# Gate and up of f-tiles 8 to 15 by seven products of halves, with sums of weights made in DRAM

## The chip, the cores and the metric

The kernel runs on one core of a Trainium2 chip. The metric is the device time of one execution in microseconds; 1120.35 us is the median of three runs of the kernel before (1120.31 to 1120.71).

## The reference

One decoder layer for 512 tokens and 1024 channels, all in float32: half a SwiGLU feed-forward added to x, two attention mixers with gates, an output projection, a second half feed-forward, a final RMSNorm. The change touches the first feed-forward only:

```python
def _swiglu(x, w_gate, w_up, w_down):
    return (jax.nn.silu(x @ w_gate) * (x @ w_up)) @ w_down

h = h + FFN_HALF * _swiglu(_rmsnorm(h, norm_ffn1[i]), ffn1_gate[i], ffn1_up[i], ffn1_down[i])
```

w_gate and w_up are 1024 x 2816, w_down is 2816 x 1024.

## The kernel before

**Layout.** Activations lie transposed: channels in partitions (8 tiles of 128, index d or k), the 512 tokens along the free dimension. The hidden width 2816 is 22 f-tiles of 128, worked in three parts (THIRDS: tiles 0 to 7, 8 to 15, 16 to 21). For each tile a gate and an up product go through TensorE, their SwiGLU is stored in G, and at the end of a third the eight output tiles of the down-projection are added to h.

**Two parts for each operand.** A float32 number is split into a high part (the cast to the matmul's type) and a low part (the rest), and a product is three matmuls: high x high, high x low, low x high. Activations are uh and ul, G holds its high parts in slots j and its low parts in slots 8+j, weights are whi and wlo. So `mm3` with 8 k-tiles is 24 matmuls, each 128 weight columns against 512 moving token columns.

**Weights.** `Weights` plans all blocks in the order of use, 512 KB each (128 x 8 x 128). A block is loaded on SP's queue into one of 4 raw buffers (`load`), split into one of 4 slots of whi and wlo (`split`: ScalarE casts, L142; VectorE subtracts, L146), and taken by `next`, which first prepares the blocks up to AHEAD = 2 further on. A load is issued three blocks ahead of the split, and waits for the split that frees its raw buffer; a cast waits for the matmuls that free its slot. Each engine runs its instructions in the order in which the program lists them.

**SwiGLU.** `swiglu` (L624 to L630, then `split`): z = gate x r_b (the norm's factor) on VectorE, Silu on ScalarE, t = up x r_b and g = s x t on VectorE, the high part of G on ScalarE (L379), the low one on VectorE (L380).

**Between the tiles.** After each tile `side` does a step of small tables (masks, rope tables) and `early` a step for twelve blocks of w_in that are used much later: load to a buffer of their own (eraw), cast and split (L103, L104), store both parts to DRAM. There is one block in each of the three stages at a time. Steps come after each tile and twice in each of the first two down-projections.

**PSUM.** `acc(False)` gives banks named acc, o, s in turn; each name has two buffers. The first matmuls of the mixing stage take both buffers of o, then both of s.

Of the kernel before, what the change touches and what calls it, by code (L numbers as in the profile page):

```python
# [59 lines left out]
class Weights:  # L60
# [19 lines left out]

    def plan(self, ap, nk, early=False, wide=False):
# [44 lines left out]
    def load(self, n):  # L126
        while len(self.raw) <= n and len(self.raw) < len(self.blocks):
            if len(self.raw) in self.stored:
                self.raw.append(None)
                continue  # L130
            ap, nk = self.blocks[len(self.raw)]
            t = self.raw_pool.tile([128, 8, 128], F32, name="raw")
            wide = self.wide[len(self.raw)]
            self.nc.sync.dma_start(t.rearrange("p (a b) c -> p a (b c)", a=2) if wide else t[:, :nk], ap)
            self.raw.append(t)
# [218 lines left out]
def layer(ctx, tc, a, out):  # L354
# [56 lines left out]


    def plan_ffn(n, begun=0, rows=()):
        for f0, f1 in THIRDS:
            for f in range(max(f0, begun), f1):
                for w in ("gate", "up"):
                    W.plan(cols(a[f"ffn{n}_{w}"], DFF, 0, KD, f * 128, 128), KD)
            if rows and f1 < NF:
                for m, g in STEPS:
                    W.plan(quarter(f0, m, g), 8, wide=True)  # L420
                continue
# [143 lines left out]
    def norm_in(d, norm):  # L565
# [4 lines left out]
        square(d)  # L570

    def square(d):
        if d == 0:
            scalar.activation(sqacc, h[:, d], AF.Square)
        else:
            sq = temp.tile([128, S], F32, name="turn_a")
            scalar.activation(sq, h[:, d], AF.Square)  # L577
# [44 lines left out]
    def swiglu(pg, pu, j):  # L622
# [8 lines left out]
        split(G[:, j], G[:, 8 + j], g)  # L631

    def ffn(after, begun, side, sums, early):

# [6 lines left out]
        def rows():  # L641
            norm_rows(norm["col"])
            for j, b in enumerate(begun):
                swiglu(*b, j)

        for third, (f0, f1) in enumerate(THIRDS):
            for f in range(f0 + (len(begun) if f0 == 0 else 0), f1):
                first = f == len(begun)
# [3 lines left out]
                mm3(pu, W.next(), u_in, KD, rows if first else None)  # L652
                swiglu(pg, pu, f - f0)
                next(side, None)
                next(early, None)
            for d in range(KD):
# [4 lines left out]
                vector.scalar_tensor_tensor(h[:, d], po, 0.5, h[:, d], op0=OP.mult, op1=OP.add)  # L661
                if third < 2 and d in (2, 5):
                    next(early, None)
                if third == 2:
                    after(d)


    hd = tc.dram_tile([KD, 128, S], F32, name="hd")

    with pool("h1") as h_pool, pool("temp1", 2) as temp, pool("tables") as tables, ExitStack() as starting:  # L670
# [108 lines left out]
        starting.close()  # L779
        with pool("stage", 2) as stage:  # L780
            ffn(to_mix, begun, side_work(), sums=sums0, early=W.early(stage))


    with ExitStack() as mixing:
        temp = mixing.enter_context(pool("temp2", 2))
# [950 lines left out]
```

## Time and profile before

| | |
|---|---|
| profiled execution | 1120.31 us, span 1118.5 us |
| TensorE (PE) busy | 1103.9 us, 99% of the span |
| VectorE (DVE) busy | 677.5 us, 61% |
| ScalarE (ACT) busy | 473.2 us, 42% |
| GpSimd (POOL) busy | 168.0 us, 15% |
| transfers | 163.16 MB, 146 GB/s in the mean |
| gate and up of f-tiles 8 to 15 | 142.71 to 229.75 us |

In a row of a timeline stand start, duration, engine, line, operation, output <- input; in brackets the idle time before it and what ended it. A row of the chain has start, duration, engine, tile, line and count. The row of a window has its length and, for TensorE's matmuls, its weight loads, VectorE, ScalarE and GpSimd, the busy time and the number of instructions; then the clock, the share of the DMA engines and GB/s. The row of a group has its count, busy time and mean in ns. An instruction of VectorE or ScalarE lasts a little longer than the distance to the next one, since its end overlaps the next one's start.

### The profile page before, as it was taken

The numbers are of one execution on the slowest core, as the hardware profiler recorded it, in microseconds if no ns is written. First come the engines' busy times: TensorE is split into PE (matmuls) and PEld (weight loads), VectorE is DVE, ScalarE is ACT, GpSimd is POOL, SyncE is SP. The second block draws the span as 40 slices with busy tenths as digits, with TensorE's granted clock in tenths as the row PEclk, the third lists the DMA queues.
The fourth block names the chain that finished last, engine by engine and source line by source line (L and its number), as shares of the span: only waits on it lengthen the run. The fifth ranks groups of instructions, "written<-read, shape, count | busy, mean of one in ns | idle before, by whom it ended". The sixth has DMA issues, their size and how long they took to land.

```text
span 1118.5 us, 14865 instructions
## 1 busy us (share of the span) xinstructions
PE 1103.9 (99%) x5571; PEld 933.1 (83%) x5571; DVE 677.5 (61%) x1243; ACT 473.2 (42%) x890; POOL 168.0 (15%) x189
## 2 busy tenths in 40 slices
PE   9999999999999999999999999999999999999997
PEld 7888888888888999998888888888888888888876
DVE  5665447543446578996777546653667754685553
ACT  5444223321234456666666543434334322342332
POOL 0100000000001145654334422120000000000002
PEclk9999999999999999999999999999999999999999
DMA  7387557533225547656658455633234623354312
GB/s 232 95 245 248 185 173 240 171 113 105 84 80 153 139 119 180 161 151 198 197 155 250 108 161 162 173 88 111 76 113 142 196 78 113 111 177 126 91 61 76
DMA packets 200577, 163.16 MB, mean 146 GB/s; under 512 B 6325, under 2 KB 177145, under 8 KB 200441
## 3 DMA queue, kind: packets, MB, share of 16 engines
q1 hardware_dynamic: 192392, 141.09, 41.9%
q0 software_dynamic: 5440, 16.78, 6.6%
q10 hardware_dynamic: 2672, 4.35, 1.0%
q8 instruction: 44, 0.72, 0.3%
q14 instruction: 29, 0.23, 0.1%
HBM read 142.27 MB, written 36.70 MB: 160 GB/s over the span
## 4 chain that ended last, share of the span: by engine, by line
PE 95%; DVE 2%; ACT 1%; issue 1%; POOL 0%; POOLq 0%; DVEq 0%; ACTq 0%
PE acc L376 37%; PE o L376 27%; PE s L376 27%; PE tp L1427 2%; DVE turn_a L1125 0%; PE tp L376 0%; PE tp L1053 0%; PE tp L718 0%; DVE wlo L146 0%; ACT whi L142 0%; PE tp L1624 0%; PE tp L985 0%; DVE s L1333 0%; POOL sqacc L578 0%; DVE sqacc L1170 0%
## 5 line engine op out<-in xcount | busy, mean ns | idle before, releaser
L146 DVE TENSOR_TENSOR wlo<-raw,whi 128x1024 fp32r<-128x1024 f32 (+2 forms) x189 | 214.6, 1163 | 42.3 <-ACT whi L142 42.2
L142 ACT CAST whi<-raw 128x1024 fp32r<-128x1024 f32 (+2 forms) x214 | 190.2, 918 | 109.8 <-PE acc L376 41.7
L376 PE MATMUL acc<-uh,whi 128*128 128x512 f32 x336 | 133.4, 397 | 0.7 <-ACT turn_a L1244 0.7
L376 PE MATMUL acc<-uh,wlo 128*128 128x512 f32 x336 | 131.3, 391 | 0.0
L376 PE MATMUL acc<-ul,whi 128*128 128x512 f32 x336 | 131.1, 390 | 0.0
L376 PE MATMUL o<-uh,whi 128*128 128x512 f32 x264 | 103.7, 393 | 0.5 <-ACT whi L723 0.4
L376 PE MATMUL o<-ul,whi 128*128 128x512 f32 x264 | 102.8, 389 | 0.0
L376 PE MATMUL o<-uh,wlo 128*128 128x512 f32 x264 | 102.8, 389 | 0.0
L376 PE MATMUL s<-uh,whi 128*128 128x512 f32 x232 | 90.5, 390 | 0.0
L376 PE MATMUL s<-uh,wlo 128*128 128x512 f32 x232 | 90.3, 389 | 0.0
L376 PE MATMUL s<-ul,whi 128*128 128x512 f32 x232 | 90.3, 389 | 0.0
L376 PEld LDWEIGHTS acc<-uh,wlo 128*128 128x128 f32 x336 | 63.1, 188 | 13.9 <-DVE wlo L146 0.4
L578 POOL TENSOR_TENSOR sqacc<-sqacc,turn_a 128x512 f32<-128x512 f32 x14 | 18.2, 1300 | 371.1 <-ACT turn_a L577 371.1
L376 PEld LDWEIGHTS acc<-uh,whi 128*128 128x128 f32 x336 | 63.1, 188 | 12.9 <-ACT turn_a L1244 1.1
L376 PEld LDWEIGHTS acc<-ul,whi 128*128 128x128 f32 x336 | 63.2, 188 | 11.9
L376 PE MATMUL acc<-whi,uh 128*128 128x256 f32 x224 | 65.6, 293 | 1.2 <-ACT whi L142 1.2
L379 ACT CAST G<-g 128x512 fp32r<-128x512 f32 x28 | 17.4, 622 | 111.5 <-DVE g L630 82.3
L376 PE MATMUL acc<-wlo,uh 128*128 128x256 f32 x224 | 63.3, 283 | 0.1
L376 PE MATMUL acc<-whi,ul 128*128 128x256 f32 x224 | 63.3, 282 | 0.0
L376 PEld LDWEIGHTS o<-uh,whi 128*128 128x128 f32 x264 | 49.6, 188 | 11.4 <-ACT whi L723 0.9
L376 PEld LDWEIGHTS o<-uh,wlo 128*128 128x128 f32 x264 | 49.5, 188 | 10.5
L376 PEld LDWEIGHTS o<-ul,whi 128*128 128x128 f32 x264 | 49.6, 188 | 10.3
(342 smaller groups left out, 2320.7 us busy)
## 6 DMA issues: line engine op xcount, KB each, us to landing
raw<-in_ffn_gate_dram SPq DMA_DIRECT2D x42, 512.0 KB, 4.0
raw<-in_ffn_up_dram SPq DMA_DIRECT2D x42, 512.0 KB, 5.2
raw<-in_ffn_down_dram SPq DMA_DIRECT2D x34, 512.0 KB, 4.7
t<-in_ffn_down_dram POOLq DMA_DIRECT2D x12, 1024.0 KB, 9.4
raw<-in_w_in_dram SPq DMA_DIRECT2D x20, 512.0 KB, 4.2
raw<-t SPq DMA_DIRECT2D x16, 512.0 KB, 4.4
eraw<-in_w_in_dram SPq DMA_DIRECT2D x12, 512.0 KB, 7.3
early<-ehi SPq DMA_DIRECT2D x12, 512.0 KB, 5.2
```

The lines of the kernel that those rows point to most:

```text
L142: self.nc.scalar.copy(self.place(i)[0][:, k0:k1], self.raw[i][:, k0:k1])
L146: engine.tensor_tensor(lo, self.raw[i][:, k0:k1], f32(hi), op=OP.subtract)
L376: tensor.matmul(out, lhsT, rhs, start=start, stop=stop)
L379: scalar.copy(hi, src)
L578: gpsimd.tensor_tensor(sqacc, sqacc, sq, op=OP.add)
L1427: tensor.transpose(ps[:w, hd], u.p[:, hd, kb * w:kb * w + w], ident)
```

## The change

Tiles 8 to 15 are worked in four units of two tiles. In a unit the matrix of weights is cut in four (gate and up, each by the two halves of the 1024 channels: g0, g1, u0, u1; 256 columns), u is cut in four (the halves of the channels by the halves of the tokens), and the four blocks of the result come from seven products of sums of these, each of 4 k-tiles, 2 column tiles, 3 parts and 256 moving columns: 24 matmuls. `unit` works them in the order 1, 6, 5, 2, 7, 3, 4 in three banks, adds further products into a bank where the sum allows, and combines the banks on VectorE.

- Three products take gate or up weights as they are, four take sums (s1 to s4) that `unit_sums` makes in DRAM: for each group of four tiles eight transfers on GpSimd's queue, 1 MB each, four of them adding into their target. `sums_of_u` makes the sums of u (split in two parts, tiles bhi and blo) while tiles 4 to 7 are worked.
- A unit takes 7 weight blocks (4 k-tiles by 256 columns) where two tiles took 4; AHEAD is 3 within units.
- The low parts of a unit's G are left to the start of the next (`settle`), or to after the last unit's early step.
- The early blocks lose eraw and go through the 4 raw buffers. Their steps come after the last two units, in the down-projection behind them, in the last third and its first two outputs. Side steps also run in the first down-projection.
- The scratch for GpSimd's DMA descriptors is 8192 where it had its default.

```diff
+UNITS = {1: (8, 16)}
+PRODUCTS = 1, 6, 5, 2, 7, 3, 4
+CHUNK = 4
@@ Weights.early @@
-            raw[n] = pool.tile([128, nk, 128], F32, name="eraw")
+            raw[n] = self.raw_pool.tile([128, nk, 128], F32, name="raw")
@@ new: unit_sums @@
+        for f, nf in chunks(UNITS[n]):
+            g0, g1, u0, u1 = (half(n, what, kh, f, nf) for what in ("gate", "up") for kh in range(2))
+            s1, s2, s3, s4 = (sum_tile(n, f, k) for k in range(1, 5))
+            for o, i, add in ((s1, u0, 0), (s3, g0, 0), (s1, u1, 1), (s3, u0, 1), (s2, s1, 0), (s2, g0, 1), (s4, s2, 0),
+                              (s4, g1, 1)):
+                if add:
+                    gpsimd.dma_start(o, i, accum_op=OP.add)
+                else:
+                    gpsimd.dma_start(o, i)
+                yield
@@ new: sums_of_u(n, k), k = 0..3 @@
+        b, p, q = (temp.tile([128, 2, 256], F32, name=name) for name in "zst")
+        scalar.activation(b[:, 0], h12, AF.Identity, scale=g1)
+        scalar.activation(b[:, 1], h22, AF.Identity, scale=g2)
+        vector.scalar_tensor_tensor(p[:, 0], h11, g1, b[:, 0], op0=OP.mult, op1=OP.subtract)
+        vector.tensor_tensor(p[:, 1], b[:, 1], p[:, 0], op=OP.add)
+        vector.tensor_tensor(q[:, 0], b[:, 0], b[:, 1], op=OP.subtract)
+        vector.scalar_tensor_tensor(q[:, 1], h21, g2, p[:, 1], op0=OP.mult, op1=OP.subtract)
+        for i, x in ((0, p), (2, q)):
+            split(both["hi"][:, k, i:i + 2], both["lo"][:, k, i:i + 2], x)
@@ new: unit(j) @@
+        def gated(s, x, i):
+            tt(x, s, x, op=OP.mult)
+            hi, lo = (G[:, b:b + 2, i * 256:i * 256 + 256] for b in (j, 8 + j))
+            scalar.copy(hi, x)
+            owed.append(lambda: tt(lo, x, f32(hi), op=OP.subtract))
+        for m in PRODUCTS:
+            wh, wl = W.next()
+            xh, xl = right(m)
+            ps = banks[home[m]]
+            new = m in (1, 5, 6)
+            for k in range(4):
+                for i in range(2):
+                    o, n = ps[:, i], 2 * k + i
+                    for step, (a_, x) in enumerate(((wh, xh), (wh, xl), (wl, xh))):
+                        tensor.matmul(o, a_[:, n], x(k), start=new and n == step == 0, stop=n == 7 and step == 2,
+                                      skip_group_check=True)
+            if m == 1:
+                settle()
+                scalar.activation(p, ps, AF.Identity, scale=-1.0)
+            if m == 6:
+                tt(u, ps, p, op=OP.add)
+            if m == 5:
+                tt(w, p, ps, op=OP.subtract)
+            if m == 2:
+                tt(z, ps, r0, op=OP.mult)
+                scalar.activation(z, z, AF.Silu)
+            if m == 7:
+                tt(w, ps, w, op=OP.add)
+                tt(w, w, r1, op=OP.mult)
+            if m == 3:
+                tt(u, ps, u, op=OP.subtract)
+                tt(u, u, r1, op=OP.mult)
+                scalar.activation(u, u, AF.Silu)
+            if m == 4:
+                gated(u, w, 1)
+                tt(t, ps, p, op=OP.add)
+                tt(t, t, r0, op=OP.mult)
+                gated(z, t, 0)
@@ ffn @@
+            while f < f1:
+                if lo <= f < hi:
+                    W.AHEAD = 3
+                    unit(f - f0)
+                    W.AHEAD = 2
+                    f += 2
+                    if f > hi - 4:
+                        next(early, None)
+                    continue
...
+                f += 1
+                if third == 0:
+                    if f > 4:
+                        sums_of_u(0, f - 5)
+                        next(adds, None)
+                        next(adds, None)
+                else:
+                    next(early, None)
                 next(side, None)
-                next(early, None)
+            settle()
             for d in range(KD):
...
-                if third < 2 and d in (2, 5):
+                if third == 0:
+                    next(side, None)
+                    next(adds, None)
+                if third == 1 and d % 2 == 0 or third == 2 and d < 2:
                     next(early, None)
@@ kernel @@
-    nc = bacc.Bacc("TRN2", target_bir_lowering=False, num_devices=1)
+    nc = bacc.Bacc("TRN2", target_bir_lowering=False, num_devices=1, dynamic_dma_scratch_size=8192)
```

VectorE within a tile of the second third before (wlo is a weight split, G the low part):

```order
L146 TENSOR_TENSOR wlo<-raw,whi 128x1024 x2
L624 TENSOR_TENSOR z<-o,r_b 128x512
L628 TENSOR_TENSOR t<-s,r_b 128x512
L630 TENSOR_TENSOR g<-s,t 128x512
L380 TENSOR_TENSOR G<-g,G 128x512
```

VectorE in a unit now, from the first operation on product 2 (z) to the last on product 4 (g; the tags of the tiles are p, s = u, t = w, z, g = t of the code; s<-s reads a bank named s):

```order
L745 TENSOR_TENSOR z<-acc,r_b 128x512
L149 TENSOR_TENSOR wlo<-raw,whi 128x1024
L748 TENSOR_TENSOR t<-o,t 128x512
L749 TENSOR_TENSOR t<-t,r_b 128x512
L149 TENSOR_TENSOR wlo<-raw,whi 128x1024
L751 TENSOR_TENSOR s<-s 128x512
L752 TENSOR_TENSOR s<-s,r_b 128x512
L149 TENSOR_TENSOR wlo<-raw,whi 128x1024
L721 TENSOR_TENSOR t<-s,t 128x512
L756 TENSOR_TENSOR g<-o,p 128x512
L757 TENSOR_TENSOR g<-g,r_b 128x512
L721 TENSOR_TENSOR g<-z,g 128x512
```

ScalarE over a whole unit now (whi is the cast of a weight block, z and s the Silu, G the high parts):

```order
L739 ACTIVATE p<-acc 128x512
L145 CAST whi<-raw 128x1024 x3
L746 ACTIVATE z<-z 128x512
L145 CAST whi<-raw 128x1024 x2
L753 ACTIVATE s<-s 128x512
L145 CAST whi<-raw 128x1024
L723 CAST G<-t 128x2x256
L723 CAST G<-g 128x2x256
```

Where two splits and four operations stood for a tile, a split stands after nearly every step of the combination, and the cast of that split stands behind the Silu or the cast of G on ScalarE.

VectorE from the last unit's product 4 into the down-projection now (elo is an early block's low part, h an output of the down-projection):

```order
L721 TENSOR_TENSOR g<-z,g 128x512
L107 TENSOR_TENSOR elo<-raw,ehi 128x1024
L724 TENSOR_TENSOR G<-t,G 128x2x256
L724 TENSOR_TENSOR G<-g,G 128x2x256
L807 SCALAR_TENSOR_TENSOR h<-o,h 128x512
```

The early block's low part moved ahead of the low parts of G for tiles 14 and 15; before, G's low part came right behind g.

SP's queue at the last unit now (the first w_in row is the first early block, the up row behind it the weights of that unit's product 4, s_12_3 and s_12_4 are sums):

```order
L137 DMA raw<-in_ffn_gate_dram 128x4x256
L137 DMA raw<-s_12_3_90 128x4x256
L137 DMA raw<-s_12_4_91 128x4x256
L101 DMA raw<-in_w_in_dram 128x8x128
L137 DMA raw<-in_ffn_up_dram 128x4x256
```

The early block now stands in the same ring of raw buffers, one load ahead of product 4's weights.

More of the change, by code (lines that the diff above doesn't have):

```diff
@@ L79, in __init__, with plan @@
         self.pos = 0
-    def plan(self, ap, nk, early=False, wide=False):
+    def plan(self, ap, nk, early=False, wide=0):
         if early:
@@ L410, in quarter, with half, chunks, sum_tile @@
         return dram(a["ffn2_down"], (f0 + 4 * g + j) * 128 * D + k * 512, [[D, 128], [256 * D, 2], [1, 512]])
+    def half(n, what, kh, f, nf):
+        return dram(a[f"ffn{n}_{what}"], kh * 512 * DFF + f * 128, [[DFF, 512], [1, nf * 128]])
+    def chunks(tiles):
+        return [(f, min(CHUNK, tiles[1] - f)) for f in range(tiles[0], tiles[1], CHUNK)]
+    s_sums = {(n, f + i, k): (tc.dram_tile([512, nf * 128], F32, name="s%d_%d_%d" % (n, f, k)), i) if i == 0 else (f, i)
+              for n, tiles in UNITS.items() for f, nf in chunks(tiles) for i in range(0, nf, 2) for k in range(1, 5)}
+    def sum_tile(n, f, k):
+        t, i = s_sums[n, f, k]
+        return t if i == 0 else s_sums[n, t, k][0]
+    def unit_sums(n):
+        for f, nf in chunks(UNITS[n]):
[8 more added lines that the diff above has]
+                yield
+    def unit_block(n, f, m):
+        if m in (1, 2, 4):
+            what, kh = {1: ("gate", 0), 2: ("gate", 1), 4: ("up", 1)}[m]
+            return cols(a[f"ffn{n}_{what}"], DFF, kh * 512, 4, f * 128, 256)
+        k = {5: 1, 6: 2, 7: 3, 3: 4}[m]
+        c = (f - UNITS[n][0]) % CHUNK * 128
+        return sum_tile(n, f, k).rearrange("(k p) c -> p k c", p=128)[:, :, c:c + 256]
     def plan_ffn(n, begun=0, rows=()):
+        lo, hi = UNITS.get(n, (0, 0))
         for f0, f1 in THIRDS:
             for f in range(max(f0, begun), f1):
+                if lo <= f < hi:
+                    for m in PRODUCTS if (f - lo) % 2 == 0 else ():
+                        W.plan(unit_block(n, f, m), 8, wide=4)
+                    continue
                 for w in ("gate", "up"):
@@ L419, in plan_ffn @@
                 for m, g in STEPS:
-                    W.plan(quarter(f0, m, g), 8, wide=True)
+                    W.plan(quarter(f0, m, g), 8, wide=2)
                 continue
@@ L575, in square @@
         else:
-            sq = temp.tile([128, S], F32, name="turn_a")
+            sq = temp.tile([128, S], F32, name=square_tag[0])
             scalar.activation(sq, h[:, d], AF.Square)
@@ new lines, in right, with settle, unit @@
+    def right(m):
+        if m in (1, 2, 3):
+            d, c = {1: (0, 0), 2: (4, 0), 3: (4, 256)}[m]
+            return tuple((lambda k, x=x: x[:, d + k, c:c + 256]) for x in (uh, ul))
+        i = {5: 0, 6: 1, 7: 2, 4: 3}[m]
+        return tuple((lambda k, x=both[part]: x[:, k, i]) for part in ("hi", "lo"))
+    owed = []
+    def settle():
+        for x in owed:
+            x()
+        owed.clear()
+    def unit(j):
+        banks = {n: psum.tile([128, 2, 256], F32, name=n) for n in ("acc", "o", "s")}
+        home = {1: "acc", 2: "acc", 5: "s", 3: "s", 6: "o", 7: "o", 4: "o"}
+        r0, r1 = (r_b[:, None, c:c + 256].to_broadcast([128, 2, 256]) for c in (0, 256))
+        p, u, w, z, t = (temp.tile([128, 2, 256], F32, name=name, bufs=2 if name != "p" else 1) for name in ("p", "s", "t", "z", "g"))
+        tt = vector.tensor_tensor
+        def gated(s, x, i):
[36 more added lines that the diff above has]
+                gated(z, t, 0)
@@ L665, in ffn @@
                     after(d)
+        for g in (adds, side, early):
+            for _ in g:
+                pass
     hd = tc.dram_tile([KD, 128, S], F32, name="hd")
@@ L779, in layer @@
         starting.close()
-        with pool("stage", 2) as stage:
+        with pool("stage", 2) as stage, pool("both") as sums_pool:
+            both["hi"], both["lo"] = (sums_pool.tile([128, 4, 4, 256], F32R, name=n) for n in ("bhi", "blo"))
             ffn(to_mix, begun, side_work(), sums=sums0, early=W.early(stage))
+    square_tag[0] = "turn_a"
     with ExitStack() as mixing:
```

13 lines of the change are left out of this document (11 added, 2 removed).

## The prediction

> **What bounds the kernel now.** I read the page's shares and its chain first.
>
> ```profile
> span 1118.5 us, 14865 instructions
> PE 1103.9 (99%) x5571; PEld 933.1 (83%) x5571; DVE 677.5 (61%) x1243; ACT 473.2 (42%) x890; POOL 168.0 (15%) x189
> PE 95%; DVE 2%; ACT 1%; issue 1%; POOL 0%; POOLq 0%; DVEq 0%; ACTq 0%
> ```
>
> TensorE carries 95% of the chain, so fewer matmul microseconds are worth something only while the other engines keep up. The sum is made against this execution's own time, 1120.31 us (span 1118.5 and 1.8 around it); the median of the three runs is 1120.35. Next the chain in order of time and the windows, for f-tiles 8 to 15 and the down-projection behind them.
>
> ```profile
> 142.87 5.44 PE o L376 x24
> ...
> 224.47 5.44 PE o L376 x24
> 229.91 5.44 PE s L376 x24
> ```
> ```profile
> 142.71:229.75 87.04, 87.04 (x385) 72.07 (x384) 50.58 (x78) 28.59 (x35) 0.00 (x0) 1.00 0.62 194
> ```
>
> Sixteen groups of 24 matmuls, 5.44 us each without a gap, 87.04 us in all: 226.7 ns per 512-wide matmul. VectorE is busy for 50.6 us (58%) of it, some of that rotary-table side work and early-gate splits, ScalarE for 28.6.
>
> **The matmuls.** A unit (two f-tiles) needs 7 products of 24 matmuls with 256 moving columns, 168, where 96 of 512 stood. The 256-wide pace is taken from a projection of the next stage:
>
> ```profile
> 385.35 8.64 PE acc L376 x72
> L376 PEld LDWEIGHTS acc<-uh,whi 128*128 128x128 f32 x336 | 63.1, 188 | 12.9 <-ACT turn_a L1244 1.1
> ```
>
> 72 in 8.64 us is 120 ns each, with a weight load before every one. So a product takes 2.88 us, a unit 20.16, and before 96 x 0.2267 = 21.76: 1.60 less per unit, 6.4 over four. Bounds: 113 ns (half of the 512-wide), which gives 10.9 less, and 188 ns (the load's own row), which gives 39 more; I take 120, the same width in an unbroken run.
>
> **VectorE and ScalarE in a unit.** This decides. The rows that price a step:
>
> ```profile
> 197.31 0.69 DVE L628 TENSOR_TENSOR t<-o,r_b 128x512 f32<-128x512 f32 x1 [3.13 <-PE o L376]
> 198.10 0.69 DVE L630 TENSOR_TENSOR g<-s,t 128x512 f32<-128x512 f32 x1
> 199.49 0.69 DVE L380 TENSOR_TENSOR G<-g,G 128x512 fp32r<-128x512 f32 x1 [0.69 <-ACT G L379]
> 200.09 0.24 DVE L547 TENSOR_SCALAR m<-n 128x160 f32<-128x160 f32 x1
> ...
> 202.10 2.35 DVE L146 TENSOR_TENSOR wlo<-raw,whi 128x1024 fp32r<-128x1024 f32 x2
> 204.37 0.68 DVE L624 TENSOR_TENSOR z<-s,r_b 128x512 f32<-128x512 f32 x1
> ```
> ```profile
> 198.83 0.62 ACT L379 CAST G<-g 128x512 fp32r<-128x512 f32 x1 [3.93 <-DVE g L630]
> 199.36 1.04 ACT L103 CAST ehi<-eraw 128x1024 fp32r<-128x1024 f32 x1
> ...
> 205.15 0.63 ACT L626 ACTIVATE s<-z 128x512 f32<-128x512 f32 x1 [2.85 <-DVE z L624]
> ```
> ```profile
> 361.26 1.04 ACT L142 CAST whi<-raw 128x1024 fp32r<-128x1024 f32 x1
> 362.33 1.55 DVE L146 TENSOR_TENSOR wlo<-raw,whi 128x1024 fp32r<-128x1024 f32 x1 [0.71 <-ACT whi L142]
> ```
>
> On VectorE a 512-wide operation lets an independent one start 0.60 after it (199.49 to 200.09) and one that needs its result 0.79 after (197.31 to 198.10); two splits and the next operation take 2.27 (202.10 to 204.37), 1.13 each (1.22 for the last). ScalarE takes a result 0.04 (cast) or 0.10 (Silu) after VectorE ends, can start its next instruction 0.53 after such a one, casts a block in 1.05, and VectorE takes that 0.03 later.
>
> A unit puts on VectorE 7 splits, 7.91 us, and 13 operations. Four are followed by one that needs them (4 x 0.79 = 3.16), six are not (3.60), together 14.67. The other three (the last on product 4, z, the second s) hand a result to ScalarE, and both queues are in order: ScalarE has the cast of the next weight block queued behind the operation on that result, and VectorE has the split that needs this cast queued right behind the operation that gave it. So VectorE stands from its own result until ScalarE has done both: 0.69 + 0.04 + 0.53 + 1.05 + 0.03 = 2.34 for product 4's, 2.39 for z, 2.40 for s; 7.13 in all. One turn of this loop takes 14.67 + 7.13 = **21.8 us**, longer than TensorE's 20.16 and as long as the 21.76 of before.
>
> How far does the lead of three split blocks carry? Unit 1 starts without a backlog and TensorE keeps its pace. Counted from its start, product 2 ends at 11.52 and z begins at 11.72 (0.20, as 229.75 to 229.95 below). From z to the first operation on product 4 it is 2.39 + 1.13 + 0.79 + 0.60 + 1.13 + 0.79 + 2.40 + 1.13 + 0.60 = 10.96, so that begins at 22.68, not at 20.36; products 7 and 3 are done before their readers. From there three turns of 21.8 lead to the same place of unit 4, 88.08. TensorE in the meantime waits now and then (product 4 for the reader of 7, in its bank, first), but its own waits don't count on top: what counts is the tail.
>
> **The tail.** The first output of the down-projection reads G of tiles 14 and 15 in its last two steps. Before:
>
> ```profile
> 229.75 0.62 PE L376 MATMUL s<-G,whi 128*128 128x512 f32 x2
> ```
> ```profile
> 229.95 0.69 DVE L628 TENSOR_TENSOR t<-o,r_b 128x512 f32<-128x512 f32 x1 [4.27 <-PE o L376]
> 230.75 0.69 DVE L630 TENSOR_TENSOR g<-s,t 128x512 f32<-128x512 f32 x1
> 232.12 0.69 DVE L380 TENSOR_TENSOR G<-g,G 128x512 fp32r<-128x512 f32 x1 [0.69 <-ACT G L379]
> ```
>
> G's low part was there 3.06 after the first matmul, and matmul 23 wants it at 22 x 0.2267 = 4.99: no wait. Now tile 14 is as late as 15, so matmul 20 wants it at 4.31; and the early gate block's cast and split are queued ahead of both low parts. From the first operation on product 4: 0.79 + 0.79 + 0.73 to ScalarE, 0.53 to the early cast, 1.05 + 0.03, 1.13 for its split, 0.60 + 0.69 for the low parts: 6.34. That is 94.42 on unit 1's clock, so the down-projection stands as if it had started at 94.42 - 4.31 = 90.11, not 87.04: **3.1 us later** than before, the 6.4 gone. With no backlog the tail alone costs 0.2 + 6.34 - 4.31 = 2.2.
>
> **Loads.** A raw slot is free when its block is split, and the load that takes it lands so long after issue:
>
> ```profile
> DMA to landing us min/median/max: 2.9/4.5/10.2
> ```
>
> In the loop the shortest time from a split's end to the cast of the block four later is 7.0 us, which covers issue and landing. In unit 4 the early block that goes ahead on SP holds a slot until the tail, so product 4's block is loaded three behind: it can start 5.1 into the turn, lands about 9.7 and is split from 10.8, where the loop wants 9.7. **1.1 us** more (below 0 at 2.9, 6.8 at 10.2; I take the median). In the down-projection an early block is loaded once the one before it is split, 1.2 before the tail's wait ends; landed 5 to 7 later, and with its cast and split ahead of the next weight block's, it has that block ready some 9.5 after the wait, where TensorE wants it after 12: 2 us to spare.
>
> **Edits at nothing.** The sums of weights are 16 transfers on POOL's queue, six in sequence for each group of four tiles:
>
> ```profile
> 39.09 0.26 POOL L508 MEMSET fold<- 128x192 f32 x1
> ...
> 349.05 1.33 POOL L578 TENSOR_TENSOR sqacc<-sqacc,turn_a 128x512 f32<-128x512 f32 x1 [309.71 <-ACT turn_a L577]
> ```
> ```profile
> t<-in_ffn_down_dram POOLq DMA_DIRECT2D x12, 1024.0 KB, 9.4
> t<-t POOLq DMA_DIRECT2D x4, 7.2
> ```
>
> POOL is free from 39.35 to 349. Four at 9.4 and two at 7.2 with 1 us for each issue make 58: done near 97 and 155. SP asks for the first sum near 121, for the second group's near 171, so both are hidden by 16 us or more; beyond that each microsecond late stops SP, then TensorE, one for one. The sums of u add at most 4 us of VectorE to each of tiles 4 to 7 (six operations of no more than 0.69) where an early split of 1.22 goes and 10.88 are to be had. Sixteen fewer turns of the bank rotation put the last output before the mixing stage in bank o, which the next matmuls' second quarter needs:
>
> ```profile
> 371.39 0.70 DVE h L661
> PE tp L376 <- DVE sqacc L603: 0.4, 1, 0.4
> ```
>
> A wait of about 0.5, of which 0.4 replaces the wait that stood a little later: **0.1**.
>
> Sum: 3.1 + 1.1 + 0.1 = 4.3 later, 1120.3 + 4.3 = **1124.6 us**.
>
> On VectorE's spacing the Trainium skill's page "VectorE: DVE Perf Modes", section "The DRAIN you can't avoid", says that the next operation starts only when the pipe is empty, whether or not it waits for a semaphore. The rows disagree: 0.60 after an operation of 0.69, and 0.79 where the result is needed. By the rule a turn would be 22.6 and the kernel some 2.6 us later still.
>
> **Rivals.** *TensorE's pace holds*: the lead covers all four units and only the tail shows. -6.4 + 2.2 + 0.1 gives 1116.2. For it speaks that VectorE's own work is 14.7 of 20.16; against it that the three hand-overs are fixed by the order of both queues. *The loop sets the end but is 4% shorter*, 20.9 a turn: 2.7 less, and the late block's 1.1 absorbed, which gives 1120.8. For it speaks that each step is priced from a stage where the engines were half idle; against it that the rows repeat to 0.02. *Loads come late in the units*, where a block is asked for every 3.1 us and not every 5.44, through one queue: it decides from a landing of about 6.6, and at 8.6 costs 2 in each of three turns on top of my sum, 1130.6, slower. For it the maximum of 10.2; against it the median. *The weight load does not hide under a 256-wide matmul*: 0.120 + 0.188 for each of 672, 207 us for 87, near 1240. The 72 in 8.64 leave no room for it. The rule behind this one stands in the Trainium skill, "TensorE: Matmul & The Clock Gate", Part 3 under "What overlaps and what doesn't": a weight load overlaps a running matmul only in another row group, and here all are in the same; this trace does not agree.
>
> **How the numbers follow.** My forecast 0.56 (by itself 1122.8 to 1127.2), TensorE's pace 0.14, the shorter loop 0.19, late loads 0.10, unhidden weight loads 0.01. A measurement of this kernel tells about 0.2% (2.2 us) from no change. Slower: 0.55 of the first, late and unhidden loads, 0.66; same: the shorter loop and 0.01 of the first, 0.20; faster: TensorE's pace, 0.14. The range 1117.5 to 1128.5 leaves out most of TensorE's pace and half of the late loads, about 0.19.
>
> **What would show it.** In the changed kernel's timeline: VectorE idle for some 1.7 us three times in each unit, each ended by ScalarE's whi cast; first operations on product 4 about 21.8 apart; TensorE's unit 1 in 20.2 us, then waits before product 4; a wait of 5 us or more inside the first output of the down-projection, ended by VectorE's low part of G; casts that wait for a transfer only in unit 4. Four units in 20.2 each with no wait but the tail's 2 us, or a 256-wide pace other than 120 ns, would prove the sum wrong.

## The result

The changed kernel takes **1133.57 us** (median of four runs: 1130.95, 1131.49, 1135.64, 1136.86) against 1120.41: a ratio of 1.0118, with a 95% interval of 1.0086 to 1.0151. It is slower, as forecast, but by 13.2 us and not 4.3, and outside the range. The profiled execution took 1131.49 us, 11.2 more than that of the kernel before. One run of e4_early_only below, 1849 us at a mean granted clock of 0.56, is left out of that kernel's figures.

### The profile page after: what moved, and what is told of

It is laid out like the page before. It is cut to its first block, busy times and chain, and to the rows that moved or that the text cites. A ratio compares the mean times of both kernels' runs of the same rounds, so it can differ in the third digit from the quotient of the medians.

```text
span 1129.7 us, 15623 instructions
## 1 busy us (share of the span) xinstructions
PE 1103.9 (98%) x5859; PEld 946.0 (84%) x5859; DVE 716.6 (63%) x1299; ACT 495.2 (44%) x922; POOL 181.3 (16%) x205
## 4 chain that ended last, share of the span: by engine, by line
PE 87%; DVE 6%; ACT 2%; DMA 2%; issue 2%; ACTq 0%; POOLq 0%; DVEq 0%
PE acc L379 32%; PE s L379 23%; PE o L379 23%; PE tp L1581 2%; PE o L735 2%; DVE wlo L149 2%; PE acc L735 2%; PE s L735 1%; ACT whi L145 1%; DMA pc<-in_positions_dram 1%; PE tp L379 1%; DMA raw<-in_ffn_down_dram 1%; DVE turn_a L1279 0%; DVE h L807 0%; PE tp L1207 0%
## 5 line engine op out<-in xcount | busy, mean ns | idle before, releaser
L149 DVE TENSOR_TENSOR wlo<-raw,whi 128x1024 fp32r<-128x1024 f32 (+2 forms) x201 | 230.6, 1171 | 62.2 <-ACT whi L145 61.9
L379 PE MATMUL acc<-uh,whi 128*128 128x512 f32 x296 | 117.7, 398 | 0.0
L379 PE MATMUL acc<-ul,whi 128*128 128x512 f32 x296 | 115.5, 390 | 0.0
L379 PE MATMUL o<-uh,whi 128*128 128x512 f32 x208 | 82.0, 394 | 0.4 <-ACT whi L875 0.4
L379 PE MATMUL o<-ul,whi 128*128 128x512 f32 x208 | 81.0, 390 | 0.0
L379 PE MATMUL o<-uh,wlo 128*128 128x512 f32 x208 | 81.0, 389 | 0.0
L379 PEld LDWEIGHTS acc<-ul,whi 128*128 128x128 f32 x296 | 55.7, 188 | 10.4
L1596 DVE TENSOR_TENSOR pts<-tp,pts 128x512 fp32r<-128x512 f32 (+1 forms) x62 | 41.8, 687 | 21.1 <-ACT pts L1593 20.4
L379 PE MATMUL o<-G,whi 128*128 128x512 f32 x156 | 49.4, 397 | 4.9 <-DVE G L724 2.6
L1495 ACT ACTIVATE pbuf<-s,m 128x256 f32<-128x256 f32 (+3 forms) x96 | 47.6, 503 | 7.7 <-DVE c L1505 4.1
L379 PE MATMUL acc<-G,whi 128*128 128x512 f32 x164 | 50.5, 389 | 0.0
```

The lines of the kernel that those rows point to most:

```text
L149: engine.tensor_tensor(lo, self.raw[i][:, k0:k1], f32(hi), op=OP.subtract)
L379: tensor.matmul(out, lhsT, rhs, start=start, stop=stop)
L1495: scalar.activation(u.p[:, hd], b.view[:, j], AF.Exp, bias=u.m[:, hd:hd + 1], scale=-1.0, accum_out=u.sum[:, hd:hd + 1])
L1596: vector.tensor_tensor(p.lo, flat(b.ps)[:w], f32(p.hi), op=OP.subtract)
```

## The profile after

The page, shares and chain:

```profile
span 1129.7 us, 15623 instructions
PE 1103.9 (98%) x5859; PEld 946.0 (84%) x5859; DVE 716.6 (63%) x1299; ACT 495.2 (44%) x922; POOL 181.3 (16%) x205
PE 87%; DVE 6%; ACT 2%; DMA 2%; issue 2%; ACTq 0%; POOLq 0%; DVEq 0%
```

TensorE is as long busy as before although its work is shorter (below: some of it runs at half clock). And 8 points of the chain have gone from TensorE to VectorE, ScalarE, transfers and the issue of instructions. To see where, I read one kind of row in every profile: VectorE's addition of an output to h, which stands at fixed places of the program. Differences to the kernel before, in us, at five places (the additions that end the first, second and last down-projection, one inside the second, and the first one of w_out, behind the mixing stage):

```
                  first down,  second down,  second down,  last down,  w_out,
                  8th output   3rd output    8th output    8th output  1st output
before (at us)      142.91       246.27        273.47        371.39     714.74
changed kernel      +1.47        +5.44         +5.44         +8.43      +11.09
```

So there are four losses: 1.5 in the first down-projection, 4.0 in the units and the tail behind them, 3.0 in the last down-projection, 2.7 in the mixing stage.

**First down-projection.** VectorE's timeline of the changed kernel, then the corresponding row before:

```profile
107.13 0.06 DVE L560 MEMSET pc<- 128x1 int32 x1
115.59 0.15 DVE L565 CAST p<-pc 128x1 f32<-128x1 int32 x1 [8.32 <-DMA pc<-in_positions_dram]
...
116.02 1.22 DVE L149 TENSOR_TENSOR wlo<-raw,whi 128x1024 fp32r<-128x1024 f32 x1
```
```profile
158.77 0.15 DVE L521 CAST p<-pc 128x1 f32<-128x1 int32 x1 [2.02 <-DMA pc<-in_positions_dram]
```

A transfer of 0.1 KB for the rotary tables, which the moved side work issues here. Before, VectorE stood 2.02 us for it; now 8.32, and the split of a weight block is queued behind. The windows say why:

```profile
99.00:142.70 43.70, 42.48 (x188) 34.86 (x187) 25.35 (x52) 12.04 (x14) 3.06 (x4) 1.00 1.01 249
```

The DMA engines are full (share 1.01), with the sums of weights among the rest; in the kernel before the share is 0.65 over the same stretch and 0.08 around the transfer at 158.77. TensorE had 1.2 us of wait from it.

**The units and the tail.** First operations on product 4, VectorE's timeline, then the tail:

```profile
166.60 0.68 DVE L756 TENSOR_TENSOR g<-o,p 128x512 f32<-128x512 f32 x1
...
188.04 0.69 DVE L756 TENSOR_TENSOR g<-o,p 128x512 f32<-128x512 f32 x1
...
209.47 0.68 DVE L756 TENSOR_TENSOR g<-o,p 128x512 f32<-128x512 f32 x1
...
229.78 1.23 DVE L149 TENSOR_TENSOR wlo<-raw,whi 128x1024 fp32r<-128x1024 f32 x1 [1.64 <-ACT whi L145]
...
231.52 0.68 DVE L756 TENSOR_TENSOR g<-o,p 128x512 f32<-128x512 f32 x1
...
235.29 1.22 DVE L107 TENSOR_TENSOR elo<-raw,ehi 128x1024 fp32r<-128x1024 f32 x1 [1.63 <-ACT ehi L106]
...
237.03 0.68 DVE L724 TENSOR_TENSOR G<-g,G 128x512 fp32r<-128x512 f32 x1
```

21.44 and 21.43 apart, then 22.05. In each turn VectorE stands three times 1.63 to 1.64 us for ScalarE's cast. TensorE's side of the tail, and the window behind it:

```profile
234.36 0.79 PE L379 MATMUL o<-G,whi 128*128 128x512 f32 x1 [2.30 <-ACT G L723]
237.77 0.79 PE L379 MATMUL o<-G,whi 128*128 128x512 f32 x1 [2.62 <-DVE G L724]
```
```profile
237.70:241.00 3.30, 3.23 (x8) 2.56 (x9) 0.70 (x2) 0.00 (x0) 0.00 (x0) 0.50 0.98 259
```

After the waits the granted clock is 0.50 for 3.3 us, which costs another 1.65. (It had fallen behind the first of the two waits already; the last section has the rows.)

**Last down-projection.** VectorE's timeline, the changed kernel; then rows of the kernel before:

```profile
347.31 1.23 DVE L107 TENSOR_TENSOR elo<-raw,ehi 128x1024 fp32r<-128x1024 f32 x1 [0.26 <-ACT ehi L106]
348.45 1.82 DVE L149 TENSOR_TENSOR wlo<-raw,whi 128x768 fp32r<-128x768 f32 x2
350.19 0.68 DVE L807 SCALAR_TENSOR_TENSOR h<-acc,h 128x512 f32<-128x512 f32 x1
353.74 1.23 DVE L107 TENSOR_TENSOR elo<-raw,ehi 128x1024 fp32r<-128x1024 f32 x1 [2.87 <-ACT ehi L106]
...
356.48 0.69 DVE L807 SCALAR_TENSOR_TENSOR h<-o,h 128x512 f32<-128x512 f32 x1
...
360.61 0.68 DVE L807 SCALAR_TENSOR_TENSOR h<-s,h 128x512 f32<-128x512 f32 x1
```
```profile
343.40 0.69 DVE L661 SCALAR_TENSOR_TENSOR h<-o,h 128x512 f32<-128x512 f32 x1
...
347.00 0.68 DVE L661 SCALAR_TENSOR_TENSOR h<-s,h 128x512 f32<-128x512 f32 x1
...
351.13 0.68 DVE L661 SCALAR_TENSOR_TENSOR h<-acc,h 128x512 f32<-128x512 f32 x1
...
355.27 0.68 DVE L661 SCALAR_TENSOR_TENSOR h<-o,h 128x512 f32<-128x512 f32 x1
```

The first addition is 6.79 later than before (5.44 were there already), since an early split stands ahead; the second is 9.48 later, since the next early block's cast waited for its load. From there each output takes 4.13 (356.48 to 360.61), and TensorE's own pace is 18 x 0.2267 = 4.08: nothing is caught up in the six outputs that follow, except for 1.0 at the end, where before the last addition had 0.97 of room.

**Mixing stage.** A wait of TensorE from the view of waits, a second one 110 us in from its timeline, and three windows, two around the first and one behind the second:

```profile
PE o L379 <- DVE h L807: 2.2, 1, 2.2
```
```profile
490.20 1.09 PE L379 MATMUL s<-ks_t,G 128*128 128x256 f32 x4 [1.77 <-ACT pbuf L1495]
```

```profile
376.00:380.50 4.50, 1.41 (x7) 0.81 (x5) 3.49 (x4) 1.43 (x3) 1.40 (x2) 1.00 0.54 165
380.50:384.80 4.30, 4.24 (x23) 4.24 (x24) 0.76 (x2) 2.22 (x5) 2.36 (x3) 0.60 0.69 183
...
490.10:493.80 3.70, 3.60 (x19) 3.21 (x20) 2.74 (x12) 1.83 (x10) 1.82 (x3) 0.54 0.00 0
```

TensorE is idle for most of 376 to 380.5, since the stage cannot begin before the late outputs, and its first 23 matmuls then run at a clock of 0.60 where 36 of 120 ns would have fitted. By the end of this first projection (its last 72 matmuls end at 403.88, before at 393.99) the kernel is 9.89 behind, 1.46 more than at the last addition. The second place is told at the end.

## The experiments

Theory after this reading: three separate losses, each with a cause that can be taken out alone (the order of hand-overs in the units; the small transfers beside the sums; early steps in the last down-projection). The times are medians over the runs named, the places those of the table above.

```
                  us (lowest to highest, runs)    1st down  2nd, 3rd  2nd, 8th  last, 8th  w_out
changed kernel    1133.6 (1131.0 to 1136.9, 4)     +1.47     +5.44     +5.44     +8.43    +11.09
e1_order          1123.3 (1119.0 to 1128.2, 9)     +5.78     -0.69     -0.69     +2.34     +6.50
e2_rope           1131.4 (1130.6 to 1132.7, 4)     +0.04     +5.37     +5.37     +8.85    +11.64
e3_spread         1137.1 (1129.8 to 1140.2, 6)     +6.46    +11.02    +11.02    +15.25    +17.05
e4_early_only     1124.7 (1123.1 to 1126.4, 4)      0.00      0.00      0.00     +3.71     +6.20
c1_order_rope     1120.5 (1116.5 to 1121.8, 11)    +0.01     -6.46     -6.46     -3.47     -2.34
c2_spread         1114.4 (1114.0 to 1115.7, 5)     -0.01     -5.77     -5.77     -5.77     -5.95
c3_bank           1116.3 (1114.9 to 1116.8, 5)     -0.03     -6.50     -6.50     -6.50     -5.46
c4_early_clear    1120.3 (1119.8 to 1120.6, 11)    -0.03     -0.03     -0.03     -0.03      0.00
d1_old_order      1131.1 (1130.3 to 1132.3, 4)     +0.49     +9.77     +9.77     +9.77    +11.96
d2_no_sums        1114.8 (1113.8 to 1116.7, 5)     -0.07     -5.56     -5.56     -5.56     -3.35
d3_no_rope        1117.1 (1114.5 to 1121.8, 12)    +6.73     +0.70     +0.38     +0.38     +0.67
```

### The order of the hand-overs (e1_order)

```diff
@@ gated @@
-            scalar.copy(hi, x)
+            owed.append(lambda: scalar.copy(hi, x))
@@ unit: for m in PRODUCTS, behind W.next() @@
+            if m == 7:
+                scalar.activation(z, z, AF.Silu)
+            if m == 4:
+                scalar.activation(u, u, AF.Silu)
@@ ffn, behind the last unit, ahead of the early step @@
+                    if f == hi:
+                        settle()
```

(and the two Silus are gone from m == 2 and m == 3.)

> Edit: in a unit the two Silus are queued on ScalarE behind the next block's whi cast, and the casts of G wait with their low parts for the next unit's first product; after the last unit they go ahead of the early block. Same work. Theory (the loop of both in-order queues, 21.4 us a turn in the trace, sets units 2 to 4): VectorE's turn falls to about 16.5 us, TensorE keeps 20.16 in all four units, the first output of the down-projection ends about 80.6 + 5.4 + 0.5 after the units start instead of 96.1, that is 8 to 9.5 us earlier, less about 1 where the early block's raw slot is missed: 1122.5 to 1125. Rival (units are paced by the raw ring, whose loads take 4.4 to 5.8 us to land): the same casts wait for the same loads, 1131 to 1134 as the changed kernel.

1123.3, a ratio of 1.0025 (1.0008 to 1.0042). From the first down-projection's end to the second's third output it is 6.47 **under** the kernel before, where the changed kernel is 3.97 over: 10.4 us by the order of instructions alone. VectorE's first operations on product 4 in this kernel:

```profile
169.02 0.68 DVE L758 TENSOR_TENSOR g<-o,p 128x512 f32<-128x512 f32 x1
...
189.16 0.68 DVE L758 TENSOR_TENSOR g<-o,p 128x512 f32<-128x512 f32 x1
...
209.30 0.68 DVE L758 TENSOR_TENSOR g<-o,p 128x512 f32<-128x512 f32 x1
...
229.44 0.68 DVE L758 TENSOR_TENSOR g<-o,p 128x512 f32<-128x512 f32 x1
```

20.14 apart each time, TensorE's own pace, with the same loads through the same ring: the rival falls. The runs spread over 9 us, and this profile has lost 5.78 in the first down-projection, where the changed kernel's lost 1.47.

### The small transfers (e2_rope, c1_order_rope, d3_no_rope)

```diff
@@ rope_tables @@
-        inv = p.tile([128, 32], F32, name="inv")
-        nc.scalar.dma_start(inv, ...)
-        pc = p.tile([128, 1], I32, name="pc")
-        ...
+        inv, pc = rope_in
@@ at the start, behind load_rest() @@
+        load_rope()
```

> Edit: the two small transfers that the rotary tables need (inv_freq and positions) are issued at the program's start, not inside the first down-projection. Theory: VectorE no longer stands 8 us for them at 107.5 to 115.5 while the sums fill the DMA engines; the units start at 142.7 as before, not 144.3, and the 1.6 us reach the end: 1.6 below the changed kernel, about 1130 (1129.5 to 1132). Rival (TensorE waits there for weight blocks that come late through the same full DMA engines, and VectorE's wait is only ahead of them): no change, 1131 to 1134.

1131.4, runs within 2.1 us. The first down-projection loses nothing now, and VectorE's row for the cast stands 0.07 behind its neighbour:

```profile
107.19 0.16 DVE L561 COPY p<-cols_c 128x4 f32<-128x4 f32 x1
107.26 0.14 DVE L562 CAST p<-pc 128x1 f32<-128x1 int32 x1
```

But in the units this profile loses 5.33 and the changed kernel's 3.97, so against 1131.49 no gain is to be seen at the end; against the median of 1133.57 it is 2.2. By itself this run doesn't decide. Two others do, where the units no longer wait. With both edits:

> Edit: the later place of the hand-overs in the units and the early issue of the two small rotary transfers, together. Theory: the two gains add and the spread between runs goes with the small transfers, since in three profiles VectorE stood 8 to 13 us for them and nothing else differed up to the units: units 6.4 under the kernel before, 3.0 to 3.7 lost in the last down-projection, 1.5 to 4 in the mixing stage: 1118.5 to 1121, and all runs within 2 us. Rival (the spread of 9 us between runs of the later hand-overs alone comes from the weight loads of the units): still 5 us or more between its runs.

1120.45, a ratio of 0.9993 (0.9984 to 1.0003): the two gains add. The spread is still 5.3 us where I had said 2: the small transfers weren't its only source. It is not shown to be the units' weight loads, as the rival has it: in this profile TensorE does not wait once in the units. The last section has what the spread goes with. And with the rest mended, but the small transfers back:

> Edit: the best so far with the two small rotary transfers back inside the first down-projection, beside the sums. Theory: this alone brings back 1.5 to 6.5 us and a spread of about 5 between runs, since each microsecond that VectorE stands past the room of 6 us there reaches the end: 1116 to 1121. Rival (in the changed kernel it was the sum of two waits, and the small transfers alone are hidden): 1114.4 within 1, little spread.

1117.1 against 1114.4, with a spread of 7.2 us where there was 1.7. VectorE's row in its profile:

```profile
119.26 0.15 DVE L565 CAST p<-pc 128x1 f32<-128x1 int32 x1 [12.04 <-DMA pc<-in_positions_dram]
```

The same transfer held VectorE 8.32, 11.1, 11.3 and 12.04 us in four profiles, and the end of the first down-projection was late by 1.47, 5.78, 6.46 and 6.73. That the changed kernel's two longer runs (1135.64 and 1136.86) are of this kind is likely: their mean granted clock (0.994 and 0.992) is that of the two shorter ones (0.994 and 0.992), so it isn't the clock that they lost by; but they have no profile. That the sums are what holds these transfers up is read from the share of the DMA engines alone: no run has the transfers at this place without the sums.

### Early steps in the last down-projection (e4_early_only, c4_early_clear, e3_spread, c2_spread)

The edit to the early blocks alone, on the kernel before:

```diff
-            raw[n] = pool.tile([128, nk, 128], F32, name="eraw")
+            raw[n] = self.raw_pool.tile([128, nk, 128], F32, name="raw")
@@ ffn, after a gate tile @@
-                next(early, None)
+                if third == 2 or f in (13, 15):
+                    next(early, None)
@@ ffn, after an output @@
-                if third < 2 and d in (2, 5):
+                if third == 1 and d % 2 == 0 or third == 2 and d < 2:
                     next(early, None)
```

> Edit: the kernel before, with only the early blocks moved to the changed kernel's places and into the raw ring; no Strassen unit, no sums. Theory: this costs what the changed kernel loses in the last down-projection, 3.7 to 4.5, and nothing elsewhere: 1124 to 1125. Rival (the last down-projection is late in the changed kernel only because it enters it with a backlog from the units): 1120 to 1121.

1124.7, a ratio of 1.0038 (1.0025 to 1.0051). Nothing is lost up to the last down-projection, then 3.71 there and 2.5 in the mixing stage: a backlog from the units is not needed. With the steps of the last down-projection moved to two more gate tiles of the second third:

```diff
-                if third == 2 or f in (13, 15):
+                if third == 2 or f in (9, 11, 13, 15):
-                if third == 1 and d % 2 == 0 or third == 2 and d < 2:
+                if third == 1 and d % 2 == 0:
```

> Edit: the kernel before, with the early blocks through the raw ring and in later places as the changed kernel has them, but four in gate tiles of the second third and none in the last down-projection; no Strassen unit. Theory: the price of that edit, 4.4 us, is all due to the two steps in the last down-projection and the last gate tile's split: 1120.4, within 0.5. Rival (the raw ring or the later stages by themselves cost, through loads that come late): 1122 to 1125.

1120.3, a ratio of 0.9998 (0.9989 to 1.0007). The raw ring and the later stages cost nothing; the 4.5 us are those two steps and the split of the last gate tile.

On the changed kernel I first moved them in another way, with two steps behind one tile:

```diff
@@ ffn, after a gate tile of the last third @@
                     next(early, None)
+                    if f == f0 + 2:
+                        next(early, None)
@@ ffn, after an output @@
-                if third == 1 and d % 2 == 0 or third == 2 and d < 2:
+                if third == 1 and (d % 2 == 0 or d == KD - 1):
```

> Edit: the early steps end before the last down-projection: one more at the end of the second third, two at tile 17, none in the last down-projection, and the last gate tile's step only stores. Theory: the changed kernel loses 3.7 us between the last gate/up group and the mixing stage, because an early split (1.1) and a wait for an early block's transfer (2.9) go into queues whose turn per output (4.14) is as long as TensorE's (4.08), so nothing is caught up; without them that is back, with up to 0.7 of the slower first matmuls of the mixing stage: 1126.5 to 1128. Rival (the extra transfers only move: more bytes at the end of the second third and in tile 17 make weight blocks late there): 1130 to 1134.

1137.1, not what I had said. The last down-projection itself is as long as before now (27.98 us from its first to its last addition, 27.99 before), but the same loss sits in the gate tile with two steps:

```profile
308.30 1.06 ACT ehi L106
...
309.38 1.24 DVE elo L107
...
310.64 6.24 DMA raw<-in_w_in_dram
...
316.98 1.05 ACT ehi L106
```

In this kernel's chain the second step's load starts only when the first step's split has freed a raw buffer, and both queues stand for it. The rival was right on the outcome, and its reason (too many bytes) can have a part: the load takes 6.24 us, where 4.4 is the median of such loads in the changed kernel. So I gave each tile one step at most, on top of the two other edits:

```diff
@@ ffn, behind a unit @@
-                    if f > hi - 4:
-                        next(early, None)
+                    next(early, None)
@@ ffn, after an output @@
-                if third == 1 and d % 2 == 0 or third == 2 and d < 2:
+                if third == 1 and d % 2 == 0:
```

> Edit: as the one before, and the early steps now one after each unit, four in the second down-projection and one per gate tile of the last third, so that the last gate tile only stores and the last down-projection has none. Theory: VectorE has room in the units now (16.5 of 20.16 us, 1.13 more for an early split), so nothing is lost there, and the 3.0 to 3.7 of the last down-projection are back, with part of what the mixing stage lost by being entered late: 1114 to 1116, 3.5 to 6 under the one before. Rival (early blocks cost the units as much as the last down-projection, through the raw slot that they hold): no gain, 1118 to 1121.

**1114.4, a ratio of 0.9947 (0.9934 to 0.9959)**, faster than both kernels, all five runs within 1.7 us. Between the second and the last down-projection nothing is lost any more.

### What is left (c3_bank, d1_old_order, d2_no_sums)

The bank of the last output:

```diff
@@ ffn, ahead of the outputs, on c2_spread @@
             settle()
+            turn[0] += third == 2
             for d in range(KD):
```

> Edit: as the one before, and the rotation of banks skips one ahead of the last down-projection, so that its last output lies in bank s as in the kernel before. Theory (the first matmuls of the mixing stage stood 2.2 us for the read of bank o and then ran at 214 ns instead of 120): 0.5 to 1.5 under the one before. Rival (they stood because the last output was late, and the clash by itself is the 0.1 of the forecast): no difference, within 0.3.

1116.3, no gain (1.9 over the median of c2_spread; where this comes from, the profiles don't show). TensorE's waits at the start of the mixing stage, with the last output in bank o (c2_spread), and in bank s (c3_bank):

```profile
PE o L379 <- DVE h L807: 0.4, 1, 0.4
```
```profile
PE tp L379 <- DVE sqacc L646: 0.4, 1, 0.4
```

One wait of 0.4 for another, so where the stage is entered on time the clash costs nothing. With a late entry it was not taken out alone. But e4_early_only, which is late there too and has its last output in bank s, loses 2.5 us in the mixing stage where the changed kernel loses 2.7, with waits of 1.19 and 1.17 at the start against 0.92 and 2.24: the late entry makes most of it, and the clash at most 0.8.

The hand-overs put back in c2_spread (the diff of e1_order undone, all else kept):

> Edit: the best so far (later hand-overs, early rotary transfers, early steps spread) with the hand-overs put back as the changed kernel has them; all else stays. Theory: the loop is back, 21.4 us a turn plus 1.1 for the early split that now stands in each of the four units: the first output of the down-projection ends 4 to 6 us later than in the kernel before where it now ends 6 earlier: 1124.5 to 1127.5, 10 to 13 over the best. Rival (the order in the units is worth little once the rest is mended, since the down-projection behind them has room to catch up): under 1120.

1131.1, 16.7 over c2_spread and more than I had said: the loop is back and turns in 21.9, 24.2 and 24.0 us, where 22.5 was said. ScalarE's timeline has what I left out:

```profile
198.79 1.05 ACT L145 CAST whi<-raw 128x1024 fp32r<-128x1024 f32 x1 [4.19 <-DMA raw<-in_ffn_up_dram]
```

With an early step in the loop a raw buffer is held by the early block, a load is issued late, and its block is waited for; VectorE stands 1.54 for it where it had none. Without the loop the same steps cost the units little: against c1_order_rope's -6.46 the table has -5.77 (c2_spread), -5.56 (d2_no_sums) and -6.50 (c3_bank).

The sums of weights left out of c2_spread (four products read plain blocks instead, so the units' result leaves the sums out):

```diff
-        adds = unit_sums(1)
+        adds = iter(())
@@ unit_block, for the products that read a sum @@
-        return sum_tile(n, f, k).rearrange(...)[:, :, c:c + 256]
+        return cols(a[f"ffn{n}_{what}"], DFF, kh * 512, 4, f * 128, 256)
```

> Edit: the best so far without the sums of weights: the four products that want them read plain gate and up blocks, the 16 transfers on GpSimd's queue are left out, so what the units compute is left wrong. Theory (the forecast's edit at nothing): the sums lie beside matmuls altogether once the small transfers are out of their way: the same time, 1114.4 within 1. Rival (they slow weight loads on the whole way from 39 to 140 us): 1 to 4 us less.

1114.8, as with them (1114.4). Its profile is a run of 1116.65; the 2.2 us that it loses in the mixing stage are looked at in the last section.

## Why the prediction was right and wrong

**The matmuls: right.** 120 ns at 256 columns gave 20.16 us for a unit; 20.14 in e1_order, and 6.47 us for four units, there and in c1_order_rope, where 6.4 were said.

**VectorE's loop: right.** Said: first operation on product 4 at 22.68 of unit 1, then every 21.8. Measured: 22.43 (166.60, where unit 1 started at 144.17), then 21.44 and 21.43. Most of the difference is the price of a dependent operation, four of them in a turn: 0.72 (L756 to L757) where I took 0.79 from a single pair. The rest is in the three waits, up to 0.08 shorter each. Taking the three hand-overs out of the queues' way removed the whole of it (e1_order), putting them back brought it back (d1_old_order).

Two rules of the Trainium skill were weighed there. By "What overlaps and what doesn't" (page "TensorE: Matmul & The Clock Gate", Part 3) a unit would have been 51.7 us, an estimate from 0.120 and 0.188 for each of 168 matmuls; that does not hold here. I read "The DRAIN you can't avoid" (page "VectorE: DVE Perf Modes") by half: the section says that the next operation does not start until the pipe is empty, and adds that one that is not held starts earlier. The turn of 21.4, not 22.6, and the 0.60 behind operations of 0.69 agree with the second part.

**The tail: right.** 6.34 from the first operation on product 4 to the low part of G; 6.19 measured (231.52 to 237.71).

**The late load in unit 4: right in kind,** 0.62 (22.05 less 21.43), said 1.1.

These came to 4.2 us and the place shows 3.97. This agreement flatters: by the smaller turns, load and tail it should have been about 2.2, and the half clock behind the waits, which was in no term, put 1.65 back. That the sum came out here was luck.

**The side work in the first down-projection, taken at nothing: wrong.** "Edits at nothing" prices the sums of weights, the sums of u and the bank; the side steps that the change puts into the first down-projection are in no term. Their operations on VectorE cost nothing to be seen (e2_rope, where the end of that stage is 0.04 late). The transfer that goes with them does: its row (2.02 us, with the DMA engines all but empty) was in the trace, and the forecast had itself put the sums on the DMA engines there. Measured: 1.5 in one profile, 5.8 to 6.7 in three others.

**Early blocks in the down-projections, "2 us to spare": wrong for the last one.** The working was for the second down-projection, and the trace bears it out there: e4_early_only ends that one to the hundredth with the kernel before. The last one has 18 matmuls per output, not 24, and to each output its norm's operations; its loop of h, uh, square, cast, split was 4.14 us before (351.13 to 355.27) against 4.08 of TensorE, with no room at all. Measured: 3.0 there and, since the mixing stage is entered late and its first matmuls run at low clock, 1.46 more; together 4.45; on the kernel before, without a unit, 4.5 (e4_early_only against c4_early_clear).

**The bank rotation, 0.1: right where the mixing stage is entered on time** (c3_bank). **The sums of weights at nothing: right by themselves** (d2_no_sums); what the small transfers lose beside them stands above.

**In no term:** some 1.2 us of the mixing stage's 2.7, from the second place there (the last section), and the spread between runs, which puts the median 2.1 over the profiled run.

Of the rivals, TensorE's pace was there to be had, but not with this order. Late loads came up where an early step stands in a unit (unit 4 of the changed kernel, d1_old_order). No rival was about the edits that I had taken at nothing, and they made most of the difference to the forecast: 1.5 + 3.0 + 1.5 of the 11.1 us at the last place of the table, beside the 4.0 of the units and the tail and the 1.2 in no term.

## What to carry to other kernels

An edit taken at nothing needs its own row: for every step that moves, ask what its smallest transfer waits for at the new place, and how long the loop there is against TensorE's pace. Where the two are equal, each microsecond put into the queue reaches the end. On two in-order queues that hand results to each other, let an operation that waits for the other engine be queued behind work that doesn't: here that was worth 10 us without a change in the work.

## What the runs showed of the hardware that was not expected

**A short wait can cost twice, and need not.** Behind three waits of TensorE in the changed kernel the granted clock fell to one half: behind the 2.30 us of the tail, and it stayed there through the 2.62 that followed; behind the 2.2 (a wait of 0.92 and two matmuls just ahead of it); behind the 1.77. After the 1.2 us in the first down-projection it stayed at 1.00. Windows of the three halves:

```profile
234.40:241.20 6.80, 4.18 (x9) 3.00 (x10) 3.12 (x4) 0.95 (x2) 0.00 (x0) 0.50 0.51 140
381.15:384.55 3.40, 3.40 (x19) 3.40 (x18) 0.75 (x1) 1.36 (x4) 1.80 (x2) 0.50 0.87 230
490.38:493.80 3.42, 3.42 (x19) 3.03 (x20) 2.46 (x11) 1.55 (x8) 1.82 (x3) 0.50 0.00 0
```

So the half lasted 3.4 us twice and 6.8 once, and cost some 1.7 us of work each time. The Trainium skill's page "TensorE: Matmul & The Clock Gate", Part 1, says that the clock falls to one half after an idle window of about 3.4 us and comes back after one such window of work. The half and the time to come back agree with the rows; here waits of 1.77 to 2.30 us were enough.

But the wait alone does not decide. The ten profiles with units all have the wait of 1.77 (1.76 to 1.79) in the mixing stage. Behind it the clock fell to 0.50 in six (the changed kernel, e1_order, e2_rope, e3_spread, d1_old_order, d2_no_sums) and stayed at 1.00 in four (c1_order_rope, c2_spread, c3_bank, d3_no_rope). The wait in c2_spread and a window behind it:

```profile
474.53 0.74 PE L379 MATMUL s<-ks_t,G 128*128 128x256 f32 x4 [1.77 <-ACT pbuf L1505]
```
```profile
475.30:477.30 2.00, 2.00 (x20) 1.75 (x19) 1.79 (x9) 1.11 (x7) 0.99 (x2) 1.00 0.00 0
```

Where the last down-projection had lost nothing, the table has 1.8 to 2.2 us more at w_out than at the last addition with the half clock (e3_spread, d1_old_order, d2_no_sums) and -0.2, 1.0 and 0.3 without it (c2_spread, c3_bank, d3_no_rope). What decides whether the clock falls was not tried.

**VectorE stood for GpSimd.** In the mixing stage an operation on two columns took 1.13 us where it took 0.16 before. Rows of VectorE and GpSimd, the changed kernel, then the kernel before:

```profile
483.85 1.13 DVE L1491 TENSOR_TENSOR e<-m,sink 128x2 f32<-128x2 f32 x1
```
```profile
479.93 6.29 POOL L149 TENSOR_TENSOR wlo<-raw,whi 128x512 fp32r<-128x512 f32 x5 [3.48 <-ACT whi L145]
```
```profile
473.98 0.16 DVE L1337 TENSOR_TENSOR e<-m,sink 128x2 f32<-128x2 f32 x1
```
```profile
470.29 6.34 POOL L146 TENSOR_TENSOR wlo<-raw,whi 128x512 fp32r<-128x512 f32 x5 [3.72 <-ACT whi L142]
```

GpSimd's five splits take 1.26 each; the fourth ends at 484.97 and VectorE's operation at 484.98. Before, the third ended at 474.09 and the operation at 474.14: it had come just at a boundary. The Trainium skill's page "SBUF — State Buffer", section "SBUF: two separate sides", tells of a port pair that the two engines share and that one of them holds for a whole instruction; the rows agree. TensorE waited 1.77 us here, 0.79 before, and with the clock it made some 2 us in the changed kernel; about one comes back later in the stage. All ten profiles with the units show 1.13 to 1.15 for this operation and the same wait, and the three without (the kernel before, e4_early_only, c4_early_clear) 0.16 and 0.8; why the phase of the two engines is always this one was not tried.

**Open.** c1_order_rope's eleven runs spread over 5.3 us, and they do so with the mean granted clock: 0.998 in the shortest (1116.49), 0.993 in the longest (1121.82). Span times clock, an estimate of what a run would take at full clock, lies within 2.1 us for all eleven (1111.7 to 1113.8). Which waits the clock fell behind in the longer runs is not known, since they have no profile.
